# Windowed attention in a two-layer encoder trunk: queries and two key heads projected with features on the partitions, values and the other two key heads first

## The chip, the cores and the metric

The kernel runs on one core of a Trainium2 chip and computes the whole trunk in one launch. The metric is the device time of that launch in microseconds, the median of several runs. The core has engines with an instruction queue each: TensorE (PE in the profile; PEld is its weight load), VectorE (DVE), ScalarE (ACT), GpSimd (POOL) and SyncE (SP, which here only starts transfers). Transfers (DMA) run beside them and are issued from SP's or POOL's queue.

## The reference

Two sequences, of 256 and 512 tokens with 1024 features, go through two layers with the same weights. Each layer is x + norm(mixer(norm(x))) followed by x + norm(SwiGLU(norm(x))). Layer 0 uses the mixer that the change touches, layer 1 a differential attention.

```python
def window_gqa_sink(h, w_in, w_o, sinks):        # |q-k| <= 128, 16 query heads, 4 key/value heads, 64 each
    qkv = h @ w_in                               # 1024 -> 1024 + 256 + 256
    q, k, v = jnp.split(qkv, [A_Q_DIM, A_Q_DIM + A_KV_DIM], axis=-1)
    ...
    q = apply_rope(q, cos, sin) * (HEAD_DIM ** -0.5)
    k = apply_rope(k, cos, sin)
    ...
        sc = jnp.einsum('bqkgd,bskd->bkgqs', qi, kb)
        sc = jnp.where(valid, sc, -jnp.inf)
        m = jnp.maximum(jnp.max(sc, axis=-1, keepdims=True), sink)
        e = jnp.exp(sc - m)
        p = e / (jnp.sum(e, axis=-1, keepdims=True) + jnp.exp(sink - m))
        return jnp.einsum('bkgqs,bskd->bqkgd', p, vb)
    ...
    return o @ w_o

def apply_rope(x, cos, sin):
    x1, x2 = jnp.split(x, 2, axis=-1)            # the two halves of a head's 64 features
    return jnp.concatenate([x1 * c - x2 * s, x2 * c + x1 * s], axis=-1)
```

## The kernel before

**Numbers.** A product in float32 is made of three products in a reduced format: each operand is split into a rounded part (hi) and the rest (lo), and hi·hi, hi·lo and lo·hi are summed (`product_steps`, lines 343 to 345). ACT rounds (L250 for weights, L331 for activations), DVE subtracts (L251, L332). Weights arrive as raw tiles by transfers from SP and wait in a ring of five split pairs; `take` and `free` move that ring on, and each `free` sets off a load, a rounding and a subtraction.

**Tokens.** The 768 tokens are six tiles t of 128: tiles 0 and 1 are the first sequence, 2 to 5 the second. The normalized input stands in `h_hi` and `h_lo` with features on the partitions, in two halves of 384 tokens.

**The first mixer** (`mixer_a`) runs 24 units, four groups gi (one key head, one value head, four query heads) of six tiles. A unit is 24 matmuls (8 k-steps of 3) with the tokens as the stationary side and 384 columns of weights moving: four query heads, a key head, a value head. Its result `pqa` has tokens on the partitions. At its end ACT copies the values, DVE rotates queries and key (`rope`, four operations) and ACT and DVE split them (`sp`). Two units later `turn` transposes them on PE: two transposes `tka` for the key's hi and lo parts, four `tqa` for the four heads, where the 64 hi and 64 lo features of a head share the 128 partitions; ACT copies all out of PSUM.

**Attention.** The items are the 96 pairs of a (group, tile) and one of its four heads, in the order of the units, four units behind them, one head per quarter unit. An item n does three things:

```python
if n < n_items:
    score(*items[n])
if n % 2 == 0 and 2 <= n <= n_items:
    normalize(*items[n - 2])
if 3 <= n <= n_items + 2:
    turn_e(*items[n - 3])
```

`score` is two matmuls over two or three key tiles (256 or 384 columns: tiles 3 and 4 see three), then on DVE a masked minimum with its row result (L667) and on ACT an exponential with its sum (L670). `normalize` serves two heads: the sink's term, the reciprocal and two divisions on DVE (L684). `turn_e` transposes the probabilities on PE (`tpe`, L693), and ACT copies them out (`eT`, L697). `values(i)` multiplies them with the values (`poa`, L707) and copies the result into `o`. It is called at the end of the unit behind the one that scored its tile. `weave` spreads the items evenly over a unit's eight k-steps.

**What sets the order.** Every engine works through its queue in the order in which the program issues instructions, and that order is written out by hand: unit, item and the place of `turn` behind the fourth step. Behind the 24 units come the first half of the output projection (`po0_0_t`) and the last items; the norm gains `gpre` and `gpost` are loaded at the kernel's start.

**The second mixer** (`mixer_b`) already projects its queries and keys with features on the partitions. A tile there is copied out by ACT (L832), its halves of 32 features are exchanged by four transfers from POOL (L834), DVE forms x·cos, swapped x·sin and their sum (L836 to L840), and the result is rounded by ACT and subtracted by DVE. The change takes these lines out of `mixer_b` as functions of their own; what they do there stays.

## Time and profile before

| | |
|---|---|
| median of 3 runs | 1656.42 us (1656.4 to 1659.1) |
| the profiled execution | 1656.38 us, of which the span of instructions is 1654.4 us |
| PE busy | 1618.3 us, 98% of the span, 9163 instructions |
| PE's weight loads | 1499.3 us, 91% |
| DVE | 1222.8 us, 74%, 2167 instructions |
| ACT | 934.4 us, 56%, 2038 instructions |
| POOL | 170.7 us, 10%, 275 instructions |

The page cuts the span into 40 slices of 41.4 us. Each digit is the busy share of a slice in tenths; the first six digits are the time of the first mixer, up to about 250 us:

```profile
PE   7999999899999999999999999999899999999997
DVE  7787756896766666888685886847896776656985
ACT  6777765654444444556475676766554444444553
POOL 1000001000000000001340461421000000000010
```

In that stage PE is full, DVE and ACT are busy for some seven tenths, and POOL does nothing behind the first slice. A duration in the views is that of one instruction; PE's instructions overlap, so the time that a row of matmuls costs is read from start to start.

### The profile page before, as it was taken

To read this page: it belongs to the slowest core of one execution; us is meant where nothing else is said; L and a number is where in the kernel's file an instruction comes from. 1 tells how busy PE (TensorE), PEld (TensorE's weight loads), DVE (VectorE), ACT (ScalarE), POOL (GpSimd) and SP (SyncE) were. 2 spreads that over 40 slices of the span, in tenths; PEclk is the share of its full clock that TensorE was granted. 3 is DMA by queue.
4 is the path that set the end of the run, shared out by engine and by line. 5 is a ranking of instruction groups with operands and counts; after the bars stand their busy time and mean duration, and the time that the engine had idled before them with its cause. 6 is when DMAs were issued, how large, how long until landed. Compare 5 with 4: busy or idle time off the path is not lost. (4 is left out here: it accounts for less than half of the span.)

```text
span 1654.4 us, 24784 instructions
## 1 busy us (share of the span) xinstructions
PE 1618.3 (98%) x9163; PEld 1499.3 (91%) x9163; DVE 1222.8 (74%) x2167; ACT 934.4 (56%) x2038; POOL 170.7 (10%) x275
## 2 busy tenths in 40 slices
PE   7999999899999999999999999999899999999997
PEld 7888878899999998888999999888899999998886
DVE  7787756896766666888685886847896776656985
ACT  6777765654444444556475676766554444444553
POOL 1000001000000000001340461421000000000010
PEclk9999999999999999999999999999999999999999
DMA  6111104544333337675542332504443332337664
GB/s 217 40 39 49 37 16 153 178 137 139 101 131 110 131 116 246 239 253 180 156 111 69 98 84 79 152 1 166 153 156 123 117 125 97 131 129 254 228 238 159
DMA packets 70233, 220.64 MB, mean 133 GB/s; under 512 B 9249, under 2 KB 15521, under 8 KB 69857
## 3 DMA queue, kind: packets, MB, share of 16 engines
q1 hardware_dynamic: 54576, 175.93, 31.5%
q0 software_dynamic: 15392, 42.87, 9.1%
q8 instruction: 72, 1.18, 0.3%
q14 instruction: 49, 0.39, 0.1%
q10 hardware_dynamic: 144, 0.26, 0.0%
HBM read 163.59 MB, written 42.86 MB: 125 GB/s over the span
## 5 line engine op out<-in xcount | busy, mean ns | idle before, releaser
L251 DVE TENSOR_TENSOR wlo<-wraw,whi 128x1024 fp32r<-128x1024 f32 (+2 forms) x174 | 203.1, 1172 | 184.1 <-ACT whi L250 183.2
L250 ACT CAST whi<-wraw 128x1024 fp32r<-128x1024 f32 (+2 forms) x174 | 175.9, 1013 | 124.3 <-PE py L344 59.3
L343 PE MATMUL py<-hhi,whi 128*128 128x384 f32 x464 | 155.2, 335 | 0.3 <-ACT u L1061 0.3
L345 PE MATMUL py<-hhi,wlo 128*128 128x384 f32 x464 | 155.0, 334 | 0.0
L344 PE MATMUL py<-hlo,whi 128*128 128x384 f32 x464 | 155.0, 334 | 0.0
L331 ACT CAST hhi<-araw 128x768 fp32r<-128x768 f32 (+1 forms) x74 | 57.6, 782 | 91.3 <-DMA araw<-act 84.7
L343 PE MATMUL pv<-whi,hhi 128*128 128x512 f32 (+1 forms) x240 | 92.3, 385 | 0.0
L345 PE MATMUL pv<-whi,hlo 128*128 128x512 f32 (+1 forms) x240 | 92.2, 384 | 0.0
L344 PE MATMUL pv<-wlo,hhi 128*128 128x512 f32 (+1 forms) x240 | 92.1, 384 | 0.0
L332 DVE TENSOR_TENSOR hlo<-araw,hhi 128x768 fp32r<-128x768 f32 (+1 forms) x74 | 65.3, 889 | 32.6 <-ACT hhi L331 32.2
L343 PEld LDWEIGHTS py<-hhi,whi 128*128 128x128 f32 x464 | 87.1, 188 | 0.8 <-ACT u L1061 0.6
L344 PEld LDWEIGHTS py<-hlo,whi 128*128 128x128 f32 x464 | 87.1, 188 | 0.0
L345 PEld LDWEIGHTS py<-hhi,wlo 128*128 128x128 f32 x464 | 87.1, 188 | 0.0
L1114 POOL DMA_DIRECT2D act<-st x22 | 19.4, 882 | 636.6 <-DVE st L1113 636.6
L343 PE MATMUL po<-whi,hhi 128*128 128x512 f32 x192 | 78.4, 408 | 0.6 <-ACT hhi L331 0.6
L388 POOL TENSOR_TENSOR rstd_post<-rstd_post,mhalf 128x1 f32<-128x1 f32 x23 | 20.3, 885 | 544.9 <-ACT rstd_post L387 544.9
L345 PE MATMUL po<-whi,hlo 128*128 128x512 f32 x192 | 75.4, 393 | 0.9 <-DVE hlo L332 0.9
L901 ACT ACTIVATE be<-bsc,bmx 128x512 f32<-128x512 f32 (+1 forms) x96 | 58.7, 615 | 30.6 <-DVE bmx L899 30.0
L344 PE MATMUL po<-wlo,hhi 128*128 128x512 f32 x192 | 75.2, 392 | 0.0
L343 PE MATMUL px<-hhi,whi 128*128 128x384 f32 x208 | 69.8, 337 | 3.8 <-ACT hhi L331 2.8
L344 PE MATMUL px<-hlo,whi 128*128 128x384 f32 x208 | 69.7, 335 | 2.1 <-DVE hlo L332 2.1
L343 PE MATMUL pqa<-whi,hhi 128*128 128x384 f32 x192 | 71.1, 370 | 0.0
(307 smaller groups left out, 5049.0 us busy)
## 6 DMA issues: line engine op xcount, KB each, us to landing
act<-st POOLq DMA_DIRECT2D x22, 1344.0 KB, 6.6
wraw<-in_wgu SPq DMA_DIRECT2D x56, 512.0 KB, 4.7
araw<-act SPq DMA_DIRECT2D x70, 384.0 KB, 4.0
y_wraw<-in_wgu SPq DMA_DIRECT2D x40, 512.0 KB, 3.6
wraw<-in_wd SPq DMA_DIRECT2D x40, 512.0 KB, 4.0
xd<-x SPq DMA_DIRECT2D x18, 512.0 KB, 3.0
x<-xd SPq DMA_DIRECT2D x18, 512.0 KB, 4.3
wraw<-in_wo SPq DMA_DIRECT2D x16, 512.0 KB, 3.5
```

Source lines behind the costliest of these rows:

```text
L250: state["raw_hi"] = nc.scalar.copy(out=hi, in_=src)
L251: state["raw_lo"] = nc.vector.tensor_tensor(out=lo, in0=src, in1=hi.bitcast(F32), op=ALU.subtract)
L331: state["hi"] = nc.scalar.copy(out=hi, in_=src)
L332: state["lo"] = nc.vector.tensor_tensor(out=lo, in0=src, in1=hi.bitcast(F32), op=ALU.subtract)
L343: nc.tensor.matmul(out, ah, bh, start=start and i == 0, stop=False, skip_group_check=more)
L344: nc.tensor.matmul(out, ah, bl, start=False, stop=False, skip_group_check=more)
L345: nc.tensor.matmul(out, al, bh, start=False, stop=stop and i == last, skip_group_check=more)
L388: nc.gpsimd.tensor_tensor(out=r[:, :w], in0=r[:, :w], in1=mhalf[:, :w], op=ALU.pow)
L901: nc.scalar.activation(out=e[:, :n * P], in_=s, func=AF.Exp, bias=mx, accum_out=den[:, c:c + 1])
L1114: nc.gpsimd.dma_start(out=at_hand[c // 4][:, :, c // 2 % 2], in_=out.pop(c // 2))
```

## The change

The first mixer is rewritten; the rest of the kernel keeps its work. The parts:

1. The projection is cut in another way. Six `kv` units (`straight`) hold the four value heads and key heads 0 and 1, tokens on the partitions, for one tile each. Sixteen `q` units and two `k` units (`rotated`) hold two heads each (f = 0 to 7 queries, f = 8 key heads 2 and 3) for 384 tokens, with the weights' 128 columns as the stationary side and the tokens moving. The number of units (24), of matmuls in each (24) and their width (384) stay.
2. `q` and `k` tiles are rotated where they stand (`rotate`, once the second mixer's): copy by ACT, four swaps from POOL, product, product and sum on DVE. The second part (`rest`, run by `turned`) comes behind the fifth step of the next unit. `place_q` writes the hi and lo halves of a head; `place_k` does so for keys and starts two transfers that repeat them on the other 64 partitions.
3. Only key heads 0 and 1 are still rotated by `rope` and transposed, `tka` x4 in six units.
4. The items have a new order (`a_items`: in a half of three tiles, two heads of each tile and then the other two) and positions given by a table of marks. `turn_e` follows four items behind the score instead of three; for tiles with two key tiles it puts two heads into one bank and one copy. `values` follows the tile's last `turn_e` directly (`after`).
5. `normalize` divides its second head on GpSimd.
6. The rope tables by feature are loaded into the gains' places; the two gains are loaded behind the last rotations (`gains[0]()`) and behind the loop (`gains[1]()`).

```diff
+def a_fill():
+    out = [("kv", 0, 0), ("kv", 1, 0), ("kv", 2, 0), ("q", 0, 0), ("kv", 3, 0), ("kv", 4, 0), ("kv", 5, 0)]
+    out += [("q", 1, 0), ("q", 0, 1), ("q", 1, 1)]
+    out += [("q", 2, 0), ("q", 3, 0), ("k", 8, 0), ("q", 2, 1), ("q", 3, 1), ("k", 8, 1)]
+    for g in (2, 3):
+        out += [("q", f, half) for half in range(2) for f in (2 * g, 2 * g + 1)]
+    return out
+def a_items():
+    out = [(g, t, 2 * p + c) for g in range(3) for half in range(2) for p in range(2)
+           for t in range(3 * half, 3 * half + 3) for c in range(2)]
+    out += [(3, t, j) for t in range(NT) for j in range(4)]
+    marks = ((0, 6.6), (6, 8.7), (24, 12.3), (48, 17.7), (76, 23))
+    at = [p + (q - p) * i / (n - m) for (m, p), (n, q) in zip(marks, marks[1:]) for i in range(n - m)]
+    return out, at
...
+    def rotate(ap, tab, pm, half, name, scale, place, z_bufs=2):
+        x = xpool.tile([P, 2, HALF], F32, tag="x", name=f"x{name}")
+        s, r = x[:, 0], x[:, 1]
+        nc.scalar.activation(out=s, in_=pm, func=AF.Copy, scale=scale)
+        for a in range(4):
+            nc.gpsimd.dma_start(out=r[a * 32:a * 32 + 32], in_=s[(a ^ 1) * 32:(a ^ 1) * 32 + 32])
+        z = ap.tile([P, HALF], F32, tag="z", name=f"z{name}", bufs=z_bufs)
+        state["mark"] = nc.vector.tensor_tensor(out=z, in0=s, in1=tab[0][:, half], op=ALU.mult)
+        def rest():
+            nc.vector.tensor_tensor(out=r, in0=r, in1=tab[1][:, half], op=ALU.mult)
+            nc.vector.tensor_tensor(out=z, in0=z, in1=r, op=ALU.add)
+            place(z)
+        return rest
+    def place_q(d, z):
+        for c, (rows, other) in enumerate(((UP, DOWNROWS), (DOWNROWS, UP))):
+            nc.scalar.copy(out=d[rows, c], in_=z[rows])
+        for c, (rows, other) in enumerate(((UP, DOWNROWS), (DOWNROWS, UP))):
+            nc.vector.tensor_tensor(out=d[other, c], in0=z[rows], in1=d[rows, c].bitcast(F32), op=ALU.subtract)
...
+            def rotated(kind, f, half):
...
+                steps = product_steps(pm, [
+                    (tuple(w[:, k * P:(k + 1) * P] for w in (whi, wlo)), (h_hi[half][:, k], h_lo[half][:, k]))
+                    for k in range(KT)])
...
+                        d = q[f, half] = ap.tile([P, 2, HALF], F32R, tag="q", name=f"qa{f}_{half}", bufs=3)
...
-                for c in range(2):
-                    e = blocks[i, j + c][0]
-                    nc.vector.tensor_scalar(out=e, in0=e, scalar1=den[:, c:c + 1], scalar2=None, op0=ALU.mult)
+                for c, eng in enumerate((nc.vector, nc.gpsimd)):
+                    e = blocks[g, t, j + c][0]
+                    eng.tensor_scalar(out=e, in0=e, scalar1=den[:, c:c + 1], scalar2=None, op0=ALU.mult)
...
+                heads = (j,) if nk == 3 else (j - 1, j) if j % 2 else ()
...
-                if 3 <= n <= n_items + 2:
-                    turn_e(*items[n - 3])
+                if LAG <= n < n_items + LAG:
+                    turn_e(*items[n - LAG])
+            def after(n):
+                m = n - LAG
+                return [lambda: values(*items[m][:2])] if m >= 0 and items[m][2] == 3 else []
...
+                if i < n_units - 1:
+                    fill = fill[:5] + [lambda late=late: turned(late)] + fill[5:]
+                    att, pos = [], []
+                    for n, x in enumerate(at):
+                        if i <= x < i + 1:
+                            more = [lambda n=n: item(n)] + after(n)
+                            att += more
+                            pos += [int((x - i) * len(fill))] * len(more)
+                    fill = placed(att, pos, fill)
```

Three places of the built order follow. In a row stand the line, the operation and out<-in by the program's names with their numbers; x2 is two instructions alike.

PE before, in the middle of the mixer (unit 12 of 24; `sc8_3` is the score of tile 2 of group 1, fourth head):

```order
L693 MATMUL tpe7_3_1503<-ident_81,y_e7_2_1378 128x128 x2
L637 MATMUL tka10_1509<-ident_r_86,sp10_1315 128x128 x2
L639 MATMUL tqa10_1508<-ident_r_86,sp10_1315 128x128 x4
L657 MATMUL sc8_3_1522<-kha1_2_1265,qa8_1267 128x256
L658 MATMUL sc8_3_1522<-kla1_2_1266,qa8_1267 128x256
L345 MATMUL pqa_12_1449<-whi11_1443,hlo0_112 128x384
L343 MATMUL pqa_12_1449<-whi11_1443,hhi0_110 128x384
```

PE after, where tile 1 of group 0 gets its last probabilities (`poa0_1`) and the next tiles their first scores:

```order
L753 MATMUL sc0_3_0_925<-ka0_296,qa0_1_894 128x384 x2
L753 MATMUL sc0_3_1_954<-ka0_296,qa0_1_894 128x384 x2
L794 MATMUL tpe0_1_3_959<-ident_81,y_e0_1_2_843 128x128 x4
L809 MATMUL poa0_1_965<-eT0_1_804,va0_288 64x256 x2
L809 MATMUL poa0_1_965<-eT0_1_804,va1_350 64x256 x2
L365 MATMUL pqa2_0_953<-hhi0_110,whi6_617 128x384
```

The block of six transposes of keys and queries is gone, a score reads one tile `ka` with both parts, and the products with the values stand directly behind the transposes `tpe` that give them their probabilities.

ACT after, the same place: `eT0_1` is the copy of those probabilities, which `poa0_1` reads, and `oa1` the copy of its result:

```order
L765 ACTIVATE y_e0_3_0_928,den0_3_0_930<-y_e0_3_0_928,negm0_3_0_929 128x384
L621 ACTIVATE xqa1_1_945<-pqa1_1_836 128x384
L765 ACTIVATE y_e0_3_0_928,den0_3_0_930<-y_e0_3_0_928,negm0_3_0_929 128x384
L800 COPY eT0_1_804<-tpe0_1_3_959 128x2x2x128
L772 ACTIVATE den0_3_0_930<-den0_3_0_930 128x2
L812 COPY oa1_230<-poa0_1_965 128x256
```

The copy `eT0_1` stands behind the exponential of the row `y_e0_3_0`, whose second entry is that of the score `sc0_3_1`, and behind the copy `xqa1_1` of a projected query tile.

DVE after, around the first query tile of heads 2 and 3 (`qa1_0`), which the score `sc0_0_2` reads; `zqa1_0` and `xqa1_0` are its rotation's two products:

```order
L762 ISA y_e0_2_0_726,negm0_2_0_727<-sc0_2_1_759,mask_91,nsink_107 128x256
L762 ISA negm0_2_0_727 128x1
L771 TENSOR_TENSOR den0_2_0_728<-negm0_2_0_727,sink_106 128x2
L773 TENSOR_TENSOR den0_2_0_728<-den0_2_0_728 128x2
L774 RECIPROCAL den0_2_0_728<-den0_2_0_728 128x2
L777 TENSOR_SCALAR y_e0_2_0_726<-y_e0_2_0_726,den0_2_0_728 128x256
L628 TENSOR_TENSOR xqa1_0_738<-xqa1_0_738,ropea1_433 128x384
L629 TENSOR_TENSOR zqa1_0_744<-zqa1_0_744,xqa1_0_738 128x384
L273 TENSOR_TENSOR wlo9_823<-wraw9_641,whi9_822 128x1024
L638 TENSOR_TENSOR qa1_0_779<-zqa1_0_744,qa1_0_779 64x384 x2
```

PE after, the end of the projection that stands ahead of that score:

```order
L365 MATMUL pqa0_1_746<-hhi1_111,whi4_363 128x384
L366 MATMUL pqa0_1_746<-hlo1_113,whi4_363 128x384
L367 MATMUL pqa0_1_746<-hhi1_111,wlo4_364 128x384
L753 MATMUL sc0_0_2_790<-ka0_296,qa1_0_779 128x256 x2
L753 MATMUL sc0_0_3_811<-ka0_296,qa1_0_779 128x256 x2
L794 MATMUL tpe0_1_1_816<-ident_81,y_e0_1_0_685 128x128 x4
L365 MATMUL pqa1_1_836<-hhi1_111,whi5_598 128x384
```

In the rotation's order, sum (L629) and subtraction (L638) are parted by the split of a weight tile (`wlo9`). Before the change no operation of DVE stood between a query's transposes and its scores.

POOL after, from its first swaps on (`xqa` are swaps, 32 partitions each; `y_e` the divisions):

```order
L623 DMA xqa0_0_481<-xqa0_0_481 32x384 x4
L777 TENSOR_SCALAR y_e0_0_0_626<-y_e0_0_0_626,den0_0_0_628 128x256
L623 DMA xqa1_0_738<-xqa1_0_738 32x384 x2
L777 TENSOR_SCALAR y_e0_1_0_685<-y_e0_1_0_685,den0_1_0_687 128x256
L623 DMA xqa1_0_738<-xqa1_0_738 32x384 x2
L777 TENSOR_SCALAR y_e0_2_0_726<-y_e0_2_0_726,den0_2_0_728 128x256
L623 DMA xqa0_1_828<-xqa0_1_828 32x384 x4
L777 TENSOR_SCALAR y_e0_0_2_793<-y_e0_0_2_793,den0_0_2_795 128x256
```

Before, POOL has no row at this place: its queue goes from the last `rstd_pre0` of the input norm to the first `rstd_post0` behind the mixer. Two of the four swaps of `xqa1_0` stand behind the division of `y_e0_1_0`.

## The prediction

> **What bounds the kernel now.** First the page's busy shares, then the busy time by stretches of the first mixer, then who waited for whom in it.

> ```profile
> span 1654.4 us, 24784 instructions
> ...
> PE 1618.3 (98%) x9163; PEld 1499.3 (91%) x9163; DVE 1222.8 (74%) x2167; ACT 934.4 (56%) x2038; POOL 170.7 (10%) x275
> ```
> ```profile
> 40.00:200.00 160.00, 158.53 (x1079) 139.15 (x1078) 125.86 (x473) 120.20 (x414) 0.00 (x0) 1.00 0.12 36
> 200.00:262.00 62.00, 59.89 (x314) 45.97 (x314) 37.80 (x102) 40.24 (x110) 0.00 (x0) 1.00 0.16 51
> ```

> The columns of the second block are PE, PE's weight loads, DVE, ACT and POOL. PE works in 158.5 of the 160 us in which the mixer is in full swing; DVE has 126 and ACT 120. The granted clock is 1.00. So PE sets this stage, and the time follows what is taken from PE's queue plus what PE is made to wait. It waits little today. The next rows are waits between 20 and 262 us (who, for whom, total us, times, longest):

> ```profile
> PEld tpe L693 <- DVE y_e L684: 4.0, 9, 0.9
> ...
> PE tpe L693 <- DVE y_e L684: 1.8, 4, 0.7
> PEld poa L707 <- ACT eT L697: 1.8, 5, 0.4
> ```

> Transposes of the probabilities (tpe) wait for DVE's division, and products with the values (poa) for ACT's copy. Behind the sixth tile of the first output projection the built orders of PE are the same before and after, so only the first 260 us are in question.

> **Term 1: transposes that go, -10.8 us.** PE's timeline, one block as before (start, us, what):

> ```profile
> 111.06 0.38 PE L693 MATMUL tpe<-ident,y_e 128*128 128x128 f32 x2
> 111.20 0.37 PE L637 MATMUL tka<-ident_r,sp 128*128 128x128 f32 x2
> 111.41 0.50 PE L639 MATMUL tqa<-ident_r,sp 128*128 128x128 f32 x4
> 111.74 0.41 PE L343 MATMUL pqa<-whi,hhi 128*128 128x384 f32 x1
> 111.99 0.33 PE L344 MATMUL pqa<-wlo,hhi 128*128 128x384 f32 x1
> 112.16 0.34 PE L345 MATMUL pqa<-whi,hlo 128*128 128x384 f32 x1
> ```

> Matmuls overlap, so I count from start to start. Six transposes take 111.74 - 111.20 = 0.54 us; 24 blocks take 13.0. After the change six blocks of four are left: 0.21 for the first two, then 0.083 each, 0.37; six take 2.2. The saving is 10.8; at 0.083 for each of the 120 it would be 10.0, the lower bound. The projections cost nothing: 576 products of 384 columns stand on both sides, 0.17 us from start to start, and the second mixer's, which already hold the weights' columns as the stationary side, last as long:

> ```profile
> L344 PE MATMUL pqa<-wlo,hhi 128*128 128x384 f32 x192 | 65.0, 339 | 0.0
> L344 PE MATMUL pqb<-hlo,whi 128*128 128x384 f32 x128 | 42.8, 335 | 0.0
> ```

> Scores, probability transposes and value products keep their number and sizes.

> **Term 2: waits for the division, -2.5 us.** From a pair's second score to the divided row nine operations of DVE and ACT follow each other; the rows show the first, the longest and the last. Their means (0.48, sum 0.08, 0.52, sum 0.20, 0.16, 0.21, 0.16, 0.16, 0.35) make 2.3 us:

> ```profile
> L667 DVE CUSTOM_DVE_ANT_0 y_e<-sc,mask,nsink 128x256 f32<-128x256 f32 x64 | 30.6, 479 | 9.8 <-PE sc L658 9.1
> ...
> L670 ACT ACTIVATE y_e<-y_e,negm 128x256 f32<-128x256 f32 x64 | 33.0, 516 | 6.6 <-DVE negm L667 6.6
> ...
> L684 DVE TENSOR_SCALAR y_e<-y_e,den 128x256 f32<-128x256 f32 x64 | 19.9, 350 | 0.8
> ```

> In the order before, PE has as little as 2.5 to 3.2 us of other work between that score and the transpose; after, with the lag of four items, 4.3 us or more everywhere. Of the 1.8 (matmuls) to 4.0 us (weight loads) of waiting I count 2.5 as gone.

> **Term 3: value products, +5.5 us.** Before, values() was called at a unit's end, several instructions behind the last probability transpose. After, it follows turn_e of the same tile directly. In the built order of PE 12 of 24 tiles have at most 0.6 us of work between the last transposes and the product that reads them. ACT's copy must fit in there:

> ```profile
> L697 ACT COPY eT<-tpe 128x384 f32<-128x384 f32 x32 | 15.2, 476 | 5.5 <-PE tpe L693 4.9
> L670 ACT ACTIVATE y_e<-y_e,negm 128x384 f32<-128x384 f32 x32 | 19.9, 622 | 2.9 <-DVE negm L667 2.6
> L667 DVE CUSTOM_DVE_ANT_0 y_e<-sc,mask,nsink 128x384 f32<-128x384 f32 x32 | 19.7, 614 | 8.3 <-PE sc L658 7.8
> L939 ACT COPY aT<-tpa 128x512 f32<-128x512 f32 x28 | 16.4, 584 | 8.4 <-PE tpa L937 8.4
> ```

> The copy takes 0.48 us, or 0.58 where two heads now share one (its size is that of the L939 row), and starts some 0.2 us after PE has gone on (two transposes take 0.38 us to their end, 0.14 to the next start, above). Eleven tiles wait 0.1 to 0.9 us, about 3.5 together. The place that the section on the change shows, poa0_1, waits longer, since on ACT the copy stands behind an exponential of a score issued just ahead: two reductions 1.23, exponential and its sum 0.82, copy 0.58 make 2.6 us after sc0_3_0, less 0.35 for sc0_3_1 and 0.4 for four transposes: 1.9 us. Together 5.4; bounds 2 (that place alone) and 12 (every place behind an exponential).

> **Term 4: queries that are not ready, +4 us.** A query tile now goes through DMA swaps. The second mixer shows each step:

> ```profile
> L832 ACT ACTIVATE xq<-pqb 128x384 f32<-128x384 f32 x16 | 7.9, 491 | 5.9 <-PE pqb L345 3.3 <-DMA xd<-x 2.5
> L834 POOL DMA_DIRECT2D xq<-xq x64 | 32.1, 511 | 89.0 <-ACT xq L832 49.8 <-ACT sq L956 35.2 <-ACT aT L939 1.8
> ...
> L840 DVE TENSOR_TENSOR zq<-zq,xq 128x384 f32<-128x384 f32 x16 | 8.8, 550 | 0.1
> L849 ACT CAST qb<-zq 64x384 fp32r<-64x384 f32 x32 | 16.3, 509 | 12.9 <-DVE zq L840 12.5
> L852 DVE TENSOR_TENSOR qb<-zq,qb 64x384 fp32r<-64x384 f32 x32 | 17.7, 553 | 4.1 <-ACT qb L849 3.5
> ```
> ```profile
> xq<-xq POOLq DMA_DIRECT2D x64, 48.0 KB, 2.6
> ```

> Copy 0.49; the fourth issue begins 1.5 later and lands 2.6 after that; product and sum 0.55 each; rounding 0.51; first subtraction 0.55: 6.7 us, some 7.2 with handovers (0.1 each, an estimate). PE's work between the projection's last product and the first score that reads it is 7.8 us or more for 15 of 16 tiles in the built order, and 5.5 for qa1_0 (24 products at 0.17, four score products at 0.12, which is 256/384 of that, and eight transposes). There the built order puts the split of a weight tile between sum and subtraction, and a division on POOL between the second and third swap.

> ```profile
> L251 DVE TENSOR_TENSOR wlo<-wraw,whi 128x1024 fp32r<-128x1024 f32 x9 | 11.0, 1222 | 4.2 <-ACT whi L250 4.0
> ```

> So 7.2 - 0.51 + 1.22 + 0.5 = 8.4, and PE waits about 2.8. Four tiles with 7.8 to 8.3 us (qa2_1, qa4_0, qa4_1, qa7_0) have no room for a queue; I add 1.2 for all. Bounds 0 and 9.

> **What lies beside other work.** The old rope and split are six operations of DVE per unit (first and last shown, 2.3 us together by their means).

> ```profile
> L558 DVE TENSOR_TENSOR r_a<-pqa,cos_sb 128x320 f32<-128x320 f32 x24 | 11.7, 488 | 13.3 <-ACT va L617 13.2
> ...
> L626 DVE TENSOR_TENSOR sp<-qk,sp 128x128 fp32r<-128x128 f32 x24 | 6.8, 283 | 0.0
> ```

> DVE loses 24 of these (55 us) and 48 divisions (18), and gains 18 rotations of five operations at 0.55 (50) and six short ropes (1.5 each, an estimate, 9): 14 less. ACT loses the casts of the old path, three copies of the transposes and half of the small probability copies. SP carries rope tables early, and the norm gains behind the last rotations, where the first output tile's 24 products of 512 columns (0.23 each by their width, 5.5 us) and four attention items cover the landing of a gain; uncovered, DVE would wait 1 to 2 us.

> ```profile
> gpost<-in_g_post SPq DMA_DIRECT2D x4, 512.0 KB, 5.1
> ```

> POOL was idle here and gets 76 DMA issues (0.51 each, 39 us) and 48 divisions. A division's price on POOL no row shows. The nearest are these products:

> ```profile
> L963 POOL TENSOR_TENSOR ob<-ob,rstd_sub 128x384 f32<-128x384 f32 x6 | 5.2, 860 | 0.5
> ...
> L963 POOL TENSOR_TENSOR ob<-ob,rstd_sub 128x128 f32<-128x128 f32 x6 | 2.6, 434 | 0.5
> ```

> 128 to 384 columns with two tensors read take 0.43 to 0.86 us; a division reads one, so for 256 I take 0.5, near the lower row. What they do to DVE, the second mixer shows:

> ```profile
> 968.45 1.25 POOL L963 TENSOR_TENSOR ob<-ob,rstd_sub 128x512 f32<-128x512 f32 x1
> 968.71 1.40 DVE L839 TENSOR_TENSOR xq<-xq,rope 128x384 f32<-128x384 f32 x1
> ```

> DVE's product of two SBUF tensors, 0.55 us elsewhere, ended only after POOL's product did. [...]

> **Sum.** -10.8 - 2.5 + 5.5 + 4.0 = -3.8 us. The profiled execution took 1656.4 us (1654.4 of span and 2.0 around it), as the median of the runs: 1652.6.

> **Rivals.** *All paid back*: terms 3 and 4 come to 13 instead of 9.5; 1656. For it: neither wait is covered in the printed order, and 13 is well within their bounds. Against: a wait for one chain is slack for the next. *Hidden after all*: only the two worst places wait (1.9 + 2.8) less what they share; 1656.4 - 13.3 + 3 = 1646. Against it: the copy's 0.48 us against gaps of 0.4. *Slower through POOL*: the second row of each pair is now divided behind swap issues (up to 2.0 us), behind DVE's own division (0.35) and in turn with DVE's two-input instructions (up to 1.2). From the score it takes 2.3 + 0.5 + 0.3 = 3.1 us with nothing ahead, and 6.6 with all ahead; the lag leaves 4.3 to 7. It decides if most pairs pass about 5 us; half of 48 pairs late by 0.5 us give +12, in all 1656.4 - 3.8 + 12 = 1665. That the transposes stay is excluded: the built order has no query transposes left.

> **How the numbers follow.** Forecast 0.40, all paid back 0.28, hidden 0.12, slower 0.20. What a measurement can tell from no change is about 0.2%, 3.3 us. Faster: most of the forecast's cases and all of the hidden ones, 0.47; same: the rest of the forecast and most of the payback, 0.31; slower 0.22. The range, 1645 to 1662, holds forecast, payback and hidden, and leaves out the far half of the slower cases.

> **What would show it.** No tqa rows, 24 tka transposes; PE's waits by tpe near 1 us, by poa on ACT near 5, by scores on DVE's query subtraction near 4, the longest of these at the first score of qa1_0. If POOL's divisions last over 1 us, or tpe waits for POOL by more than 5 us in all, the forecast falls. A slower stage with none of these waits would make it wrong in a way that I don't see.

## The result, and the profile after

The changed kernel takes 1675.61 us (median of 4 runs, 1674.7 to 1677.22), beside 1657.45 us (4 runs) for the kernel before: a ratio of 1.0112, 95% interval 1.0099 to 1.0124. It is 18 us slower; 1652.6 was forecast, with a range up to 1662.

The page of the changed kernel, busy shares and two of its rows of slices:

```profile
span 1675.4 us, 24756 instructions
...
PE 1623.6 (97%) x9043; PEld 1499.4 (89%) x9043; DVE 1222.6 (73%) x2098; ACT 930.4 (56%) x1943; POOL 264.0 (16%) x399
...
PE   7898999999999999999999999999999999999998
...
PEclk9899999999999999999999999999999999999999
```

PE lost 120 instructions, the transposes that went. The span of this execution is 21.0 us longer than that of the profiled one before; the medians differ by 18 us. The second row of slices is the granted clock, the share of its full clock that PE is given, in tenths; its second slice is no longer 9. The stretches of the first mixer (columns: PE, weight loads, DVE, ACT, POOL, then the clock) show both:

```profile
40.00:80.00 40.00, 34.28 (x200) 31.67 (x199) 29.92 (x94) 26.26 (x72) 13.42 (x18) 0.91 0.28 88
80.00:120.00 40.00, 38.28 (x237) 33.35 (x236) 28.15 (x98) 26.55 (x79) 20.40 (x27) 0.97 0.16 37
120.00:160.00 40.00, 33.70 (x202) 27.95 (x201) 29.05 (x90) 25.72 (x74) 21.15 (x29) 0.96 0.25 69
160.00:200.00 40.00, 35.89 (x230) 30.22 (x227) 30.76 (x110) 29.26 (x87) 17.57 (x23) 1.00 0.15 42
200.00:240.00 40.00, 36.43 (x208) 28.23 (x207) 27.92 (x87) 25.34 (x72) 15.58 (x21) 0.96 0.30 95
```

Before, PE was busy for 158.5 of the 160 us from 40 to 200; now for 142.2. DVE and ACT are less busy too (118 and 108 us against 126 and 120), so no other engine has become full. Whom PE waited for between 20 and 285 us (total us, times, longest):

```profile
PE sc L753 <- DVE qa L638: 9.8, 5, 3.5
PE poa L809 <- ACT eT L800: 5.4, 6, 2.2
PE po L365 <- ACT hhi L353: 2.8, 1, 2.8
PE poa L809 <- ACT eT L798: 1.1, 2, 0.8
PE tpe L794 <- DVE y_e L777: 1.0, 1, 1.0
PE tpe L794 <- POOL y_e L777: 1.0, 2, 0.7
```

Scores wait for the query's subtraction, value products for ACT's copy. As a matmul's recorded duration overlaps the next, what a wait costs is taken below from the intervals between the ends of PE's matmuls, less the usual interval of that form, wherever this is over 0.4 us. By that count the first mixer went as follows (us, up to the last value product, which ended at 246.9 before and at 267.9 after):

| | before | after | difference | forecast |
|---|---|---|---|---|
| transposes of queries and keys | 11.3 | 1.8 | -9.5 | -10.8 |
| waits of scores for queries | 0 | 11.3 | +11.3 | +4.0 |
| waits of value products for the copy | 0 | 7.6 | +7.6 | +5.5 |
| waits of probability transposes | 2.7 | 2.7 | 0 | -2.5 |
| waits of the output projection | 2.3 | 3.4 | +1.1 | 0 |
| matmuls at half clock | 0 | 5.9 | +5.9 | none |
| shorter waits and the rest | | | +4.6 | none |
| sum | | | +21.0 | -3.8 |

The row of shorter waits and the rest is what is left over to the 21.0 us; nothing below takes it apart.

The longest wait, that of qa1_0's first score, on PE, and the same time in stretches of 2 us:

```profile
59.41 0.34 PE L367 MATMUL pqa<-hhi,wlo 128*128 128x384 f32 x1
63.24 1.45 PE L753 MATMUL sc<-ka,qa 128*128 128x256 f32 x4 [3.48 <-DVE qa L638]
```
```profile
60.00:62.00 2.00, 0.00 (x0) 0.00 (x0) 1.65 (x3) 1.55 (x3) 1.35 (x3) 1.00 0.00 0
62.00:64.00 2.00, 0.76 (x3) 0.62 (x3) 1.71 (x3) 0.52 (x2) 1.35 (x3) 0.56 0.58 117
64.00:66.00 2.00, 2.00 (x10) 2.00 (x10) 1.52 (x6) 1.29 (x5) 0.00 (x0) 0.50 0.69 244
66.00:68.00 2.00, 2.00 (x8) 2.00 (x7) 0.86 (x5) 0.83 (x3) 0.00 (x0) 0.50 0.00 0
68.00:70.00 2.00, 2.00 (x12) 2.00 (x12) 0.88 (x4) 0.49 (x3) 0.97 (x1) 0.73 0.03 8
70.00:72.00 2.00, 2.00 (x17) 2.00 (x15) 1.04 (x5) 1.24 (x5) 0.12 (x1) 1.00 0.00 0
```

PE stood still for 3.48 us, and for the 6 us behind it worked at a clock of 0.50: 8 to 10 matmuls in 2 us, where 17 go at full speed (last row). A busy share of 2.00 hides this; the count beside it and the clock show it. Four waits of this mixer were followed by such a stretch, at 62, 79, 127 and 223 us.

The place that the prediction singled out for ACT's queue, poa0_1, on PE and on ACT:

```profile
78.21 1.08 PE L809 MATMUL poa<-eT,va 128*64 128x256 f32 x8 [2.23 <-ACT eT L800]
```
```profile
75.07 1.04 ACT L272 CAST whi<-wraw 128x1024 fp32r<-128x1024 f32 x1
76.00 0.61 ACT L765 ACTIVATE y_e<-y_e,negm 128x384 f32<-128x384 f32 x1
...
76.61 0.47 ACT L621 ACTIVATE xqa<-pqa 128x384 f32<-128x384 f32 x1
76.98 0.60 ACT L765 ACTIVATE y_e<-y_e,negm 128x384 f32<-128x384 f32 x1
...
77.58 0.57 ACT L800 COPY eT<-tpe 128x512 f32<-128x512 f32 x1
```

The copy stands behind two exponentials, as worked out, and between these stands the copy of a projected query tile (L621), which the prediction's sum for this place left out. 1.9 us were forecast, it is 2.2 idle (2.4 by the intervals).

### The profile page after: what moved, and what is told of

Same layout as the page of the kernel before. It is cut to its first block, busy times and chain, and to the rows that moved or that the text cites. A ratio compares the mean times of both kernels' runs of the same rounds, so it can differ in the third digit from the quotient of the medians.

```text
span 1675.4 us, 24756 instructions
## 1 busy us (share of the span) xinstructions
PE 1623.6 (97%) x9043; PEld 1499.4 (89%) x9043; DVE 1222.6 (73%) x2098; ACT 930.4 (56%) x1943; POOL 264.0 (16%) x399
## 4 chain that ended last, share of the span: by engine, by line
PE 63%; DVE 7%; DMA 5%; issue 3%; ACT 3%; POOL 1%; SPq 0%; DVEq 0%; ACTq 0%; POOLq 0%
PE py L366 6%; PE py L367 6%; PE py L365 6%; PE pw L367 4%; PE pw L366 4%; PE pw L365 4%; PE pv L367 2%; PE pv L365 2%; PE pv L366 2%; PE px L366 2%; PE px L367 2%; PE px L365 2%; PE bsc L990 2%; PE pob L1045 2%; DMA araw<-act 1%
## 5 line engine op out<-in xcount | busy, mean ns | idle before, releaser
L762 DVE CUSTOM_DVE_ANT_0 y_e<-sc,mask,nsink 128x256 f32<-128x256 f32 (+1 forms) x96 | 50.2, 525 | 29.6 <-PE sc L753 28.7
L777 POOL TENSOR_SCALAR y_e<-y_e,den 128x256 f32<-128x256 f32 (+1 forms) x48 | 57.5, 1198 | 90.5 <-DVE den L774 53.1
## 6 DMA issues: line engine op xcount, KB each, us to landing
wraw<-in_wgu SPq DMA_DIRECT2D x56, 512.0 KB, 4.5
y_wraw<-in_wgu SPq DMA_DIRECT2D x40, 512.0 KB, 3.6
wraw<-in_wd SPq DMA_DIRECT2D x40, 512.0 KB, 4.0
xd<-x SPq DMA_DIRECT2D x18, 512.0 KB, 3.0
x<-xd SPq DMA_DIRECT2D x18, 512.0 KB, 4.2
wraw<-in_wo SPq DMA_DIRECT2D x16, 512.0 KB, 3.9
```

The lines of the kernel that those rows point to most:

```text
L762: state["mark"] = nc.vector.tensor_tensor_reduce(out=e, in0=s, in1=mask[:, side:side + nk * P], scale=-HD ** -0.5, scalar=nsink[:, h:h + 1 ...
L777: eng.tensor_scalar(out=e, in0=e, scalar1=den[:, c:c + 1], scalar2=None, op0=ALU.mult)
```

## The experiments

Theories: PLACE (the items stand where the chains behind a projection and behind a transposition are not through yet), POOL (its divisions make everything late), CLOCK (half clock behind a wait, as a cost of its own); from run 10 on also ORDER (the queries are late for what stands ahead of them in the queues of ACT and DVE). The ratios are to the kernel before, on the same chip.

**1. e_dve: both divisions on DVE.**

```diff
-                for c, eng in enumerate((nc.vector, nc.gpsimd)):
+                for c, eng in enumerate((nc.vector, nc.vector)):
```

> Both divisions of a pair on DVE again, all else as in the changed kernel. Theory POOL (the 48 divisions on POOL, 1.09 us for 256 columns and 1.42 for 384, sit between swap issues and make queries and probabilities late): most of the 21 us goes, 1660 us or less, and the waits of scores for DVE's query subtraction fall from 11.3 to under 4 us. Theory PLACE (the chain of a query through copy, four swaps, two products, sum, rounding and subtraction is 8.5 to 14 us long against 5.5 to 10 us of PE work, whatever POOL does; the wait behind turn_e is ACT's): the swaps start about 1 us earlier at qa1_0, qa2_1, qa4_0 and qa4_1, the transposes' waits for POOL (1.5 us) go, the drop of the granted clock at 127 us goes with a wait under 2 us; 5 to 7 us in all, so about 1669 us. The wait of poa0_1 (2.4 us) stays in both.

Measured 1677.32 us, ratio 1.0124 [1.0107, 1.0141]: not faster at all. Scores wait 12.7 us, products 8.3; qa4_0, qa5_0 and qa4_1 wait 1.88, 1.47 and 1.54 us, as before to a few hundredths (1.88, 1.50, 1.54). POOL falls, though in the changed kernel its divisions cost twice what the prediction took (0.5 us) and more:

```profile
L777 POOL TENSOR_SCALAR y_e<-y_e,den 128x256 f32<-128x256 f32 x32 | 34.8, 1087 | 55.6 <-DVE den L774 34.5 <-PE tka L706 14.2 <-PE sc L753 2.9
...
L777 POOL TENSOR_SCALAR y_e<-y_e,den 128x384 f32<-128x384 f32 x16 | 22.7, 1419 | 34.9 <-DVE den L774 18.6 <-PE sc L753 6.2 <-ACT oa L812 5.5
```

PLACE had expected 5 to 7 us of gain from earlier swaps, and was wrong in that.

**2. e_fill: PE is kept busy in three of the long waits.**

```diff
+FILL = {(0, 0, 2): 30, (0, 1): 16, (1, 3, 0): 16}
...
+                for i in range(n):
+                    nc.tensor.matmul(
+                        out[:, :256], h_hi[0][:, 0, :P], h_hi[0][:, 1, :256], start=i == 0, stop=i == n - 1)
```

> 62 products of 256 columns that nothing reads are put on PE ahead of three of its longest waits (30 ahead of the score sc0_0_2, 16 ahead of the product poa0_1, 16 ahead of the score sc1_3_0), 0.12 us each, so 3.6, 1.9 and 1.9 us of extra work inside waits of 3.9, 2.4 and 2.5 us. Theory CLOCK (a wait of over about 2 us makes PE run at a granted clock of 0.50 for 3.4 to 6.8 us behind it, and that part of the loss comes on top of the wait): with PE kept busy the three drops at 62, 79 and 127 us go, the fourth at 222 us stays; 5 to 6 us faster than the changed kernel in spite of more work, about 1670 us. Rival (the drops have another cause than idle time): the drops stay, and the time is the same or up to 2 us longer.

Measured 1672.62 us, 1.0099 [1.0084, 1.0114]: 3.0 us faster than the changed kernel with 7.4 us more work on PE. The intervals of the two ratios overlap, so the gain is small beside the noise; in the one trace of each, the last value product ends 3.6 us earlier (264.3 against 267.9). The three stretches at half clock are gone, the fourth (now at 220 us) stayed. The time at which the changed kernel ran at 0.50:

```profile
62.00:64.00 2.00, 2.00 (x15) 2.00 (x16) 1.20 (x4) 0.90 (x3) 0.00 (x0) 1.00 0.03 8
64.00:66.00 2.00, 2.00 (x15) 2.00 (x14) 1.72 (x5) 2.00 (x6) 0.00 (x0) 1.00 0.00 0
```

With PE kept busy in these waits, the time at half clock up to 285 us fell from 17.1 to 3.4 us: the three stretches came from PE's idle time. The gain is half of what was expected, since the score sc0_3_0, which had not waited, now does (2.80 us idle), most likely since PE got there sooner than its query.

**3. e_shift: the items half a unit later.**

```diff
-    marks = ((0, 6.6), (6, 8.7), (24, 12.3), (48, 17.7), (76, 23))
+    marks = ((0, 7.1), (6, 9.2), (24, 12.8), (48, 18.2), (76, 23))
```

> The positions of all attention items but the last 20 are moved back by half a unit (marks 7.1, 9.2, 12.8, 18.2 in place of 6.6, 8.7, 12.3, 17.7; the last stays at 23), so that PE has 2 to 5 us more of other work between a query's projection and its first score. Theory PLACE: the waits of scores for the query subtraction fall from 11.3 to 3 us or less, and the drops of the granted clock at 62 and 127 us go with them (about 4.5 us): some 12 us faster than the changed kernel, 1663 us. Theory POOL: the denser items between 12.8 and 23 make POOL and DVE later, transposes wait instead, and the gain is under 5 us. The wait of poa0_1 and the drop behind it stay in both.

Measured 1668.64 us, 1.0076 [1.0061, 1.0091]: 7 us faster, not 12. PE's longest waits from 20 to 285 us:

```profile
PE poa L809 <- ACT eT L800: 9.3, 8, 2.2
PE po L365 <- ACT hhi L353: 3.7, 2, 3.1
PE tpe L794 <- DVE y_e L777: 3.4, 4, 1.2
PE sc L753 <- DVE qa L638: 0.9, 1, 0.9
```

The queries' waits are gone, as PLACE said; those of products and transposes grew from 10.3 to 15.9 us (by the intervals). The stretches at half clock at 62 and 127 us went, as expected; that at 79 us went too, against the expectation, and a new one of two periods stands at 166 us, among waits of a transposition and a value product.

**4. e_late: values() one item later.**

```diff
-                            more = [lambda n=n: item(n)] + after(n)
+                            more = [lambda n=n: item(n)] + after(n - 1)
```

(and `after(n0 - 1)` ahead of the first of the last units)

> values() is called one item later, so that a score and a transposition, and mostly some products of the projection, stand between a tile's last probability transposes and the product that reads their copy. If the placing right behind turn_e is what makes PE wait for ACT's copy: these waits fall from 7.6 us to 2 or less, and the drop of the clock at 79 us goes; 6 to 8 us faster than the changed kernel, about 1668 us. If ACT is behind in any case: the waits stay above 5 us, and the time moves by less than 3 us. The waits for queries stay.

Measured 1676.56 us, 1.0119 [1.0104, 1.0134]. The waits for the copy went, as expected, and the time did not move:

```profile
PE sc L753 <- DVE qa L638: 17.1, 6, 3.9
...
PE poa L809 <- ACT eT L800: 0.4, 1, 0.4
```

Seven us less for products, eight more for scores: here the one wait had been the other's slack.

**5. e_noswap: without the swaps.**

```diff
-        for a in range(4):
+        for a in range(swaps):
...
-            nc.vector.tensor_tensor(out=r, in0=r, in1=tab[1][:, half], op=ALU.mult)
+            nc.vector.tensor_tensor(out=r, in0=r if swaps else s, in1=tab[1][:, half], op=ALU.mult)
```

(`swaps` is 0 in the first mixer, 4 in the second; the kernel leaves the exchange of halves out there, so its rotation is incomplete and its output is not the trunk's)

> The four swaps of a rotated tile are left out in the first mixer, and the second product reads the copy itself (the rotation is incomplete then; all other work stays). It takes 72 transfers with their issues (0.5 us each on POOL) and some 4 us of each query's chain away. Theory PLACE (the chains of the queries are too long for the work that PE has meanwhile): the waits of scores for the query subtraction fall from 11.3 to under 3 us and the drops of the granted clock at 62 and 127 us go; the waits of value products (8 us) and transposes (3 us) stay or grow as they did when the items were moved back; 1664 to 1668 us. Rival (the chains are late for the order of DVE and ACT, and the swaps are hidden in it): the waits stay above 7 us, and the time stays within 4 us of the changed kernel.

Measured 1664.47 us, 1.0051 [1.0033, 1.007]. Scores wait 3.0 us, products 10.2: PLACE holds, and shortening the chain does what moving the items did. That it is still slower than before, with no swap at all, shows that the swaps' latency alone is not the loss.

**6. e_lag4b: the kernel before with turn_e four items behind.**

```diff
-                if 3 <= n <= n_items + 2:
-                    turn_e(*items[n - 3])
+                if 4 <= n <= n_items + 3:
+                    turn_e(*items[n - 4])
```

(and in the last units the fourth item, which stood behind the split of the output rows, now stands ahead of it)

> The kernel before with one thing of the change: turn_e follows four items behind the score instead of three (in the last units the values call moves behind the fourth item for it). The prediction's second term says that the waits of the probability transposes for DVE's division (2.7 us in the trace of before) go: 2 to 2.5 us faster than before. Rival (one wait is the slack of the next, as with the values one item later): the waits move to other places, and the time stays within 1 us of before. The later split of the output rows in the last units can cost up to 2 us in both.

Measured 1659.31 us, 1.0015 [1.0004, 1.0026]. No probability transpose waits over 0.4 us any more (2.7 before), and nothing is gained: the last value product ends 2.6 us later. PE changes between projections and value products more often (33 against 26 intervals into a group of value products from other work, 0.36 us each). That this is the whole of it was not tested, and the changed end of the mixer was not run alone.

**7. e_shift_late: both moves.** The diffs of 3 and 4 together.

> The items half a unit later and values() one item later, both at once. Alone the first took the queries' waits to 1.2 us but left 10.6 us of waits for ACT's copy, the second took those to 1.0 us but left 19 us of waits for queries. If the two kinds of wait are each other's slack but both can go at once: scores and value products together wait under 5 us, no drop of the clock before 220 us, 1658 to 1661 us. If latency on DVE and ACT is full in any case: the transposes of the probabilities wait instead (over 10 us), and the time stays at 1666 or more.

Measured 1654.86 us (10 runs), 0.9984 [0.9973, 0.9995]: 21 us faster than the changed kernel, and 0.16% faster than the kernel before (by the interval 0.05 to 0.27%).

```profile
PE tpe L794 <- DVE y_e L777: 4.7, 6, 1.8
PE sc L753 <- DVE qa L638: 2.1, 5, 1.1
PE po L365 <- ACT hhi L353: 1.7, 1, 1.7
PE poa L809 <- ACT eT L800: 1.6, 4, 0.5
```

Alone the moves gave 7 us and none; together 21. No wait before 200 us (the longest 1.8 us, of a transposition) was followed by half clock. What the transposes saved now stands against the waits: the last value product ends at 247.0 us, against 246.9 before, with 15 us of waits still in it (5.0 before).

**8. c_s8_late_tail: later still, and the end pulled forward.** Marks ((0, 7.3), (6, 9.5), (24, 13.0), (48, 18.4), (76, 23)); in the last units each item but the first, the values and the split one step earlier.

> As the one with both moves, with the items 0.7 to 0.8 of a unit later instead of half a unit, and in the last units the items and the values one step earlier, ahead of the split of the output rows. If the wait of the second output tile for ACT's rounding (3.6 us with the items moved, and a drop of the clock behind it) comes from the values being late there, it falls under 1.5 us, and the time is 2 to 4 us under that of the kernel with both moves, 1655 to 1658 us. If the end is only pressed together, waits for division and copies in the last units take it back, and the two are within 2 us.

Measured 1662.86 us, 1.003 [1.0014, 1.0046]: 8 us slower than 7, which neither side of the expectation had. Transposes wait 7.6 us and products 4.7; the second output tile still waits 3.25.

**9. Three neighbours of 7**, each with one thing changed: both divisions on DVE (c_sl_dve), `turned` behind the sixth step (c_sl_t6), the fourth mark at 18.0 (c_sl_m18).

> The kernel with the items half a unit later and values() one item later (1654.9 us), with both divisions on DVE again. If POOL's division helps once the places are right (DVE carries 0.41 to 0.44 us for each of 48 divisions, and the transposes' 7.1 us of waits are mostly for DVE): the waits of transposes grow by 2 us or more, 1657 to 1660 us. If it is as idle as it was between the changed kernel and the one with DVE's divisions (1675.6 against 1677.3): within 1.5 us.

> The kernel with both moves, and the second half of a rotation (product, sum, rounding, subtraction) is issued behind the sixth step of the next unit instead of the fifth. DVE then stands less often in front of a swap that has not landed (0.3 to 0.4 us each), and a query is ready 0.5 us later. If DVE's queue sets the 7.1 us of transposes' waits: 2 us faster, 1653 us. If the queries have no room to give: their waits grow from 3.5 to 6 us or more, and it is 1 to 3 us slower.

> The kernel with both moves, with the fourth mark at 18.0 instead of 18.2, so that the items from 48 to 76 stand 4% wider apart. If the density of items there makes the two longest waits of transposes (1.2 and 1.9 us, at 168 and 179 us): these fall under 1 us each, and the waits of the queries of group 2 grow by 1 us or less; 1 to 2 us faster. If the waits only change places: within 1 us of 1654.9 us.

Measured 1654.41 us, 0.9979 [0.997, 0.9988]; 1654.54 us, 0.9982 [0.9972, 0.9993]; 1659.67 us, 1.0008 [0.9999, 1.0018]. The first two cannot be told from 7; for the second, neither the 2 us of gain nor the 1 to 3 us of loss came. POOL's division is worth nothing here either, and with both divisions on DVE the transposes' waits fell (1.5 us against 7.1 in the one trace of each), against the expectation. The third was expected 1 to 2 us faster or the same and is about 5 us slower: qa4_0's wait rose from 0.5 to 2.75 us.

**10. e_first and c_sl_first: the query first on ACT and DVE.** In the changed kernel ACT waits while it has work. The first score of qa4_0, on PE, and ACT at the same time:

```profile
156.94 0.50 PE L753 MATMUL sc<-ka,qa 128*128 128x256 f32 x2 [1.61 <-DVE qa L638]
```
```profile
155.41 0.49 ACT L621 ACTIVATE xqa<-pqa 128x384 f32<-128x384 f32 x1 [1.79 <-PE pqa L367]
155.80 1.03 ACT L636 CAST qa<-zqa 64x384 fp32r<-64x384 f32 x2
```

The rounding of qa4_0 (L636) could have begun at 154.9, when DVE's sum was through (its rows: start 154.20, 0.72 long). But the copy of the next query tile (L621) stands ahead of it, and that waits for PE's projection to end. PE then waits for the rounding and the subtraction.

```diff
-        nc.scalar.activation(out=s, in_=pm, func=AF.Copy, scale=scale)
+        with queries_first():
+            nc.scalar.activation(out=s, in_=pm, func=AF.Copy, scale=scale)
```

(`queries_first` puts what it encloses behind the last query's roundings and subtractions; the split of a weight tile in `prepare` gets it too)

> The changed kernel with one rule for the order on ACT and DVE in the first mixer: the copy of the next projected query tile and the next weight tile's rounding and subtraction are issued behind the rounding and the subtractions of the query tile before. Theory ORDER (the queries are late for what stands ahead of them in these two queues): the wait of qa1_0 falls by the 1.2 us of the weight's subtraction, to about 2.7 us, that of qa2_1 from 2.5 to about 1, that of qa4_0 from 1.9 to under 0.5; 4 us less in all and one drop of the granted clock fewer, 1670 to 1672 us. Rival LENGTH (the chain is too long in any order): the three change by under 0.5 us each, and the time stays within 1.5 us of the changed kernel. If the later weights make the projections wait, products of the projection show waits for a weight's rounding or subtraction.

> The same rule in the kernel with the items half a unit later, values() one item later and both divisions on DVE (1654.4 us). There the score of qa7_0 waits 3.3 us, since a weight tile's rounding (1.04 us) and subtraction (1.22 us) stand ahead of the query's. Theory ORDER: that wait falls to about 1.2 us and the drop of the clock at 185 us goes, 1650 to 1652 us. Rival: what is moved behind makes the output projection's first tiles later by as much, within 1 us of 1654.4.

Measured 1671.8 us, 1.0088 [1.0071, 1.0104], and 1654.97 us, 0.999 [0.998, 0.9999]. In e_first the wait of qa4_0 is gone, ORDER being right there, but those of qa1_0 (4.1 us) and qa2_1 (2.5) stayed: for these the chain is too long in this order too. The time is in the range that ORDER gave (1670 to 1672 us), though only one of its three waits went, and its interval still overlaps that of the changed kernel. In the fast kernel (c_sl_dve, without and with the rule) the waits of scores fell from 4.5 to 2.6 us, and those of transposes rose from 1.5 to 7.6: no gain, where ORDER had 1650 to 1652 us.

Both kernels and the runs that take one cause each, with run 7, by the same count (us; waits over 0.4 us and time at half clock up to 285 us, in the profiled execution):

| | median | scores | products | transposes | output | half clock |
|---|---|---|---|---|---|---|
| before | 1657.45 | 0 | 0 | 2.7 | 2.3 | 0 |
| after | 1675.61 | 11.3 | 7.6 | 2.7 | 3.4 | 17.1 |
| e_dve | 1677.32 | 12.7 | 8.3 | 1.1 | 3.6 | 17.1 |
| e_fill | 1672.62 | 9.4 | 5.6 | 1.8 | 3.2 | 3.4 |
| e_shift | 1668.64 | 1.2 | 10.6 | 5.3 | 4.6 | 10.2 |
| e_late | 1676.56 | 19.1 | 0.6 | 5.4 | 4.1 | 20.5 |
| e_noswap | 1664.47 | 3.0 | 10.2 | 1.5 | 1.4 | 3.4 |
| e_first | 1671.80 | 9.9 | 6.5 | 1.0 | 3.9 | 17.1 |
| e_shift_late | 1654.86 | 3.5 | 2.3 | 7.1 | 2.0 | 3.4 |

## Why the prediction was wrong

- **What bounds.** That the first mixer alone is in question, and PE in it, held: the ends of the two kernels' first mixers and of their spans both differ by 21.0 us.
- **Where the time went.** Between the forecast -3.8 and the 21.0 us of the two profiled executions lie 24.8 us; by the table in the section on the result, 7.3 are from the queries, 5.9 from the clock, 4.6 from shorter waits and the rest, 2.5 from the division, 2.1 from the value products, 1.3 from the transposes and 1.1 from the output projection. For the 4.6 us no run shows a cause.
- **Term 1, transposes, -10.8.** Right. The table's -9.5 counts a block of six only to its own last end (0.47 us); from start to start, as the prediction counted, all blocks take 13.2 us before and 2.1 after, 11.1 less. The difference between the two counts stands in the table's last row but one.
- **Term 2, division, -2.5.** Wrong. The waits stayed at 2.7 us; with both divisions on DVE they are 1.1 (run 1), and with the lag alone in the kernel before (run 6) they go without a gain. The step that failed counted a wait that goes as time that is gained. It compared one chain with one cover ("in the order before, PE has as little as 2.5 to 3.2 us") and left out what else the new order moves.
- **Term 3, value products, +5.5.** Right in place and mechanism, 2.1 us too small (7.6), within its bounds.
- **Term 4, queries, +4.** The step that failed most in its size: 11.3, above the bound of 9. For qa1_0 the chain was right (2.8 forecast, 3.5 idle). For the rest "I add 1.2 for all" counted a bare chain of 7.2 us against the cover (its 0.1 us for a handover was the author's estimate; in the trace before, the first swap's issue begins 0.29 us behind the end of ACT's copy, and ACT's rounding 0.03 us behind DVE's sum); the queues of ACT and DVE made four of them wait 1.5 to 2.5 us (qa2_1, qa4_0, qa5_0 and qa4_1; of the four that were named, qa7_0 had no such wait). One of those is settled by run 10, ACT's copy of the next tile ahead of the rounding; the others' split between order and length stays open.
- **What was missing.** The sum took the clock as 1.00 because it was 1.00 before. PE had had no long wait in this stage before (none over 1.0 us by the intervals); the two longest forecast waits (1.9 and 2.8 us, in the trace 2.2 and 3.5) were both followed by half clock. This term, put at nothing without a reason, was 5.9 us; run 2 shows its cause, while its size rests on the count alone.
- **The rivals.** "Slower through POOL" had the sign and, at 1665, was nearest, but not the mechanism: the divisions are as slow as it needed (1.09 and 1.42 us in the mean, 1.99 beside the split of a weight tile) and run 1 shows that they cost nothing. So the prediction's own sign against it, divisions of over 1 us, came true without being the reason. "Against: a wait for one chain is slack for the next" was held against the rival *all paid back*. Runs 3 and 4 show what it means here: the one turned half of the queries' wait, the other all of the products', into waits of other chains, and only both together (run 7) took the loss away.
- **Worth of the change.** With its chains given room it is 0.16 to 0.21% faster than before (runs 7 and 9, 2.7 to 3.5 us). That this is near the sum of -3.8 us is luck: run 7's waits lie elsewhere than the sum had them (7.1 us of transposes, which were to lose 2.5), and the first mixer of its trace ends no sooner than before, so where the small gain arises is not shown. The positions in `marks` and the place of `values`, not the projection with features on the partitions, made the 18 us.

## What to carry to other kernels

Before a stage that is full on one engine is rearranged, work out every chain's time with the queues that it passes, and give each more cover than that: moving one wait can uncover the next, and most of the gain can appear only when both chains have room (here 7, 0, and 21 us for both moves). Where PE gets waits like those here, count a possible slower clock behind them as well: those of 2.2 and 3.5 us were followed by half clock, one of 3.6 us in e_late was not. When a transfer of work to an idle engine neither helps nor hurts, as POOL's divisions, the waiting was never for that work.

## What the runs showed of the hardware

```profile
149.00:153.00 4.00, 0.39 (x3) 0.07 (x1) 2.46 (x6) 1.51 (x3) 3.63 (x6) 1.00 0.38 88
153.00:157.00 4.00, 3.97 (x30) 2.74 (x32) 2.65 (x9) 2.35 (x8) 0.00 (x0) 1.00 0.05 12
```

So in these runs a wait cost one or two periods at half clock on top or none, by where it fell; for a period full of work that is some 1.7 us, an estimate (half of 3.41).

**In the changed kernel, where a division on POOL and a subtraction on DVE ran at once, one of the two took longer.** A division of 256 columns on POOL took 0.93 us at the least and 1.99 us while DVE split a weight tile, which took its usual 1.21 us (POOL's row, then DVE's):

```profile
116.91 1.99 POOL L777 TENSOR_SCALAR y_e<-y_e,den 128x256 f32<-128x256 f32 x1
```
```profile
116.99 1.21 DVE L273 TENSOR_TENSOR wlo<-wraw,whi 128x1024 fp32r<-128x1024 f32 x1
```

Elsewhere in the same trace DVE paid. The subtraction of a query's half took 0.55 us in the median of its 32 instructions, and up to 0.82 beside a division on POOL; one such place (POOL's row, then DVE's):

```profile
206.65 0.99 POOL L777 TENSOR_SCALAR y_e<-y_e,den 128x256 f32<-128x256 f32 x1 [2.21 <-DVE den L774]
```
```profile
206.87 0.71 DVE L638 TENSOR_TENSOR qa<-zqa,qa 64x384 fp32r<-64x384 f32 x1
```

Which of the two took longer differed from place to place, and run 1, without divisions on POOL, was no faster (1677.32 against 1675.61 us).
